# One pass over the weights for the output and query projections of a hybrid attention layer

## The chip, the core and the metric

The kernel runs on one core of one Trainium2 chip. A core has a matrix engine (TensorE, PE in the profile, with its weight loads as PEld), a vector engine (VectorE, DVE), a scalar engine (ScalarE, ACT), GpSimd (POOL) and SyncE (SP), whose queue issues most of the transfers. PE writes its results to PSUM, in banks of 512 float32 values per partition. The metric is the device time of one execution in microseconds.

## What is computed

The input is x, 2048 tokens of 1024 features. One layer is computed, with two token mixers beside each other:

```python
h = einsum("bsd,dc->bsc", x, w_in)                   # all input projections
qkv = silu(causal_short_conv(h[..., :1536], conv_w)) # branch A: gated DeltaNet, 4 heads of 128
o_a = chunked_gated_delta_rule(q_a, k_a, v_a, g, beta)
y_a = rmsnorm(o_a) * dn_norm_w * silu(dn_z)
q_b = partial_rope(sw_q); k_b = partial_rope(sw_k)   # branch B: 8 query heads of 64, window 128
y_b = banded_sink_attention(q_b, k_b, v_b, sinks) * silu(sw_z)
merged = sigmoid(gate_a) * (y_a @ w_branch[0]) + sigmoid(gate_b) * (y_b @ w_branch[1])
out = merged @ w_out
y = layer_norm(alpha * x + out) * ln_g + ln_b
```

The delta rule needs the inverse of a unit triangular matrix for each block of tokens.

## The kernel before

The 2048 tokens go through in four chunks of 512 (T), each of four blocks of 128. The order of pieces within a chunk stands in two strings, `ORDER_FIRST` for chunk 0 and `ORDER` for the others (L44, L45): "kv" and "w0", "w1" are the projections of window attention, "q0" to "v3" those of the delta rule's heads, "g" and "z" gates, and "p" a quarter of the output projection of the chunk before. So a chunk from the second on holds two query pieces (w0, w1) and four projections (p).

Every float32 product is made of three matmuls on high and low parts (`prods`, L173 to L175). Weights arrive in quarters of 512 columns as a pair of high and low parts in a buffer "wb". There are four such buffers (`W_SPLIT`). In the first use of a weight it is loaded raw, split by ScalarE and GpSimd (L154, L155) and stored back to DRAM as "kw_..."; later uses load that (L150). Where tokens are the rows of the result (`prod_tc`, L190), a quarter of the weights is the moving operand and a block of tokens the stationary one. Results stand in PSUM buffers "mm", of which there are three.

`window_q` (L538) makes the queries of four heads. It goes over its four quarters twice: first for blocks 0 and 1, then for blocks 2 and 3, each block in a PSUM buffer of its own, with the list `ww` keeping the quarters for the second pass. After each pass `rope` (L857) rotates the two blocks into SBUF tiles "kr" (a ScalarE copy, L861, and four VectorE instructions, L865 to L867), and `query_rows` (L557) is set up, which transposes them on PE (L562) into the tiles "qT". There are two "kr" buffers, so the second pair of blocks needs the transposes of the first: `st.finish("qT0")`. `project` (L666) likewise goes over its quarters twice, once for blocks 0 and 2 and once for 1 and 3, with two blocks in each of two banks.

The order on PE is written out by the program. Dense products come from generators that give their planned length (`PE_R`, 216 ns for 512 columns), and the class `Order` (L805) keeps a clock `now` of planned time. Dependent work is a task: `spawn` gives it a latency after which it may stand (`LAT_Q`, 7900 ns, for `query_rows`), and after each few products `run` puts down all tasks whose time has come. A task's step gives its own length and the latency until its next step. `finish(name)` (L834) runs tasks until one is done, and where none is ready it sets the clock forward to the next one's time:

```python
if name not in self.done:
    self.now = min(t[0] for t in self.tasks)
```

Tasks that matter here: `front` (L350; decay products L387, then the matrix m goes through DRAM to the tile "su"), `inverse` (VectorE, L904 to L916, result through DRAM to "p_", L423 and L435), `levels` (L426; its first matmuls on p_ are L447), and `back` (L472), the delta rule's recurrence: L494, then VectorE's bt (L496), L499 and L502, VectorE's wc (L501), L505 and L507, VectorE's S (L506), and so on for four blocks. The other engines' order is set by a scheduler.

Of the kernel before, what the change touches and what calls it, by code (L numbers as in the profile page):

```python
# [8 lines left out]
F32 = mybir.dt.float32  # L9
# [7 lines left out]
P = 128  # L17
D = 1024
KT = D // P
T = 512  # L20
NB = T // P
# [40 lines left out]
def build(tc, xt, xn, wk, wg, par, lnp, cst, out, seq=2048):  # L62
    nc = tc.nc
    NCH = seq // T
    with ExitStack() as ctx:
# [9 lines left out]
        sm = pool("sm", 2)  # L75
        mm = pool("mm", 3, space=PSUM)
# [5 lines left out]
        first = {}  # L82
        stage = lambda src: (lambda t: (nc.sync.dma_start(out=t, in_=src), t)[1])(ps_.tile([P, T], F32, name="s"))
        for n in ("x0", 0, "x1", 1, 2, "x2", "x3", 3, 4, 5, "x4", "x5", "x6", "x7"):
            if isinstance(n, str):
                k = int(n[1])
# [11 lines left out]
        cos = ct[:, C_COS:C_COS + P].rearrange("p (n e) -> p n e", e=8)  # L98
        sin = ct[:, C_SIN:C_SIN + P].rearrange("p (n e) -> p n e", e=8)
# [59 lines left out]
        def half_w(name, i, k=4, out=None):  # L159
            return [w.rearrange("p (k c) -> p k c", k=k) for w in split((name, i), wg[G_AT[name], :, 512 * i:512 * i + 512], 512, out)]  # L160

        def quarters(names):

            for name in names:
                for i in range(2):
                    yield half_w(name, i, 2)

        def prods(ps, terms, first=True, last=True):

            n = len(terms) - 1  # L170
            cost = PE_R * ps.free_size() / 512
            for i, (sh, sl, mh, ml) in enumerate(terms):
                nc.tensor.matmul(ps, sh, mh, start=(first and i == 0), stop=False)  # L173
                nc.tensor.matmul(ps, sh, ml, start=False, stop=False)  # L174
                nc.tensor.matmul(ps, sl, mh, start=False, stop=(last and i == n))  # L175
                if cost * 3 * (i % 2 + 1) > 1000 or i == n:
                    yield cost * 3 * (i % 2 + 1)

        def proj_ct(c, name):

            c.ps = mm.tile([P, T], F32, name="mm")
            for i in range(2):
                wh, wl = half_w(name, i)
                load_x(c, 4 * i + 3)
                yield from prods(c.ps, [(wh[:, k], wl[:, k], c.xh[4 * i + k], c.xl[4 * i + k]) for k in range(4)], i == 0, i == 1)

        def tok(a, b):
            return a[:, b * P:(b + 1) * P]

        def prod_tc(pss, blocks, ah, al, ww, load=None):  # L190

            for g, (wh, wl) in enumerate(ww):
                if load:
                    load(2 * g + 1)
                for ps, b in zip(pss, blocks):
                    yield from prods(ps, [(tok(ah[2 * g + k], b), tok(al[2 * g + k], b), wh[:, k], wl[:, k])
                                          for k in range(2)], g == 0, g == 3)

        def kept(ww, into):
            for w in ww:  # L200
                into.append(w)
                yield w

        def load_x(c, k):

            for k in range(len(c.xh), k + 1):
                if not k % 2:
                    c.pair = [px.tile([P, 2, T], F32R, name=n) for n in ("xh", "xl")]
                hi, lo = (t[:, k % 2] for t in c.pair)
                raw = pw.tile([P, 528], F32, name="w", bufs=W_RAW)[:, :512]  # L210
                nc.sync.dma_start(out=raw, in_=xt[c.i, :, k // 2, k % 2])
                nc.scalar.activation(hi, raw, AF.Copy)
                nc.vector.tensor_tensor(lo, raw, hi.bitcast(F32), ALU.subtract)
                c.xh.append(hi)
                c.xl.append(lo)
# [106 lines left out]
        def silu2(c, name):  # L322
            yield from proj_ct(c, name)
            while sum(n not in st.done for n in c.zs) >= 3:
                st.finish(next(n for n in c.zs if n not in st.done))
            c.zs.append(f"window{int(name[2]) // 2}" if name[0] == "z" else f"gate{name[1]}")
            r = ph.tile([P, T], F32, name="z", bufs=3)
            nc.scalar.activation(r, c.ps, AF.Tanh, scale=0.5)
            nc.vector.scalar_tensor_tensor(r, r, 1.0, c.ps, ALU.add, ALU.mult)
            c.z[name] = r  # L330
# [207 lines left out]
        def window_q(c, gp):  # L538

            if gp:  # L540
                st.finish("window0")
            c.qT = [pa.tile([P, NB, 2, P], F32R, name=n, bufs=1) for n in ("qT0", "qT1")]
            ww, more = [], quarters([f"q{gp}{i}" for i in range(2)])
            for b0 in (0, 2):
                pss = [mm.tile([P, T], F32, name="mm")[:, :256] for _ in range(2)]
                yield from prod_tc(pss, (b0, b0 + 1), c.xh, c.xl, ww if b0 else kept(more, ww), lambda k: load_x(c, k))
                if b0:
                    st.finish("qT0")
                qr = [pa.tile([P, 256], F32, name="kr") for _ in range(2)]
                for b, ps in enumerate(pss):  # L550
                    rope(nc, sm, qr[b], ps, 4, cos[:, c.i * NB + b0 + b], sin[:, c.i * NB + b0 + b])
                st.spawn(f"qT{b0}", query_rows(c, b0, qr), LAT_Q)
            for g in range(2):
                yield from silu2(c, f"zb{2 * gp + g}")
            st.spawn(f"window{gp}", attend(c, gp), LAT_W)

        def query_rows(c, b0, qr):  # L557

            pst = pp.tile([P, 2, 2, P], F32, name="pp")
            for b in range(2):  # L560
                for g in range(2):
                    nc.tensor.transpose(pst[:, b, g], tok(qr[b], g), ident)  # L562
            lo = pa.tile([P, 2, 2, P], F32, name="pT").bitcast(F32R)
            for v, vs_ in enumerate(HALF):
                q = c.qT[v][:, b0:b0 + 2]
                nc.scalar.activation(q[vs_], pst[vs_], AF.Copy)
                nc.vector.tensor_tensor(lo[vs_], pst[vs_], q[vs_].bitcast(F32), ALU.subtract)
                nc.gpsimd.dma_start(out=q[HALF[1 - v]], in_=lo[vs_])
            yield 4 * PE_T, 0
# [96 lines left out]
        def project(c, eg):  # L666

            if not eg:
                c.ra = [py.tile([P, 2, D], F32, name=n) for n in ("yBh", "yBl")]
            ww, more = [], quarters([f"o{eg}{i}" for i in range(2)])  # L670
            es = slice(256 * eg, 256 * eg + 256)
            xr, pss = [], [mm.tile([P, 2, 256], F32, name="mm") for _ in range(2)]
            for bp in range(2):
                xr.append(pa.tile([P, 2, 256], F32, name="s"))
                t0 = c.i * T + bp * 256
                nc.sync.dma_start(out=xr[bp], in_=xn[t0:t0 + 256, es].rearrange("(b p) e -> p b e", p=P))
            for b2 in range(2):
                yield from prod_tc([ps[:, b2] for ps in pss], (b2, 2 + b2), c.mh, c.ml, ww if b2 else kept(more, ww))
            for bp in range(2):
                nc.vector.scalar_tensor_tensor(c.ra[bp][:, :, es], xr[bp], 2.0 * ALPHA, pss[bp], ALU.mult, ALU.add)  # L680

# [97 lines left out]
        c = Chunk(0)  # L779
        for i in range(NCH):  # L780
# [20 lines left out]
            c = nxt  # L801
# [55 lines left out]
def rope(nc, sm, out, ps, heads, cos, sin):  # L857

    split = lambda a: a[:, :64 * heads].rearrange("p (h e) -> p h e", e=64)
    s, d = split(ps), split(out)  # L860
    nc.scalar.activation(d[:, :, 16:], s[:, :, 16:], AF.Copy)  # L861
    t = s[:, :, :16].rearrange("p h (r e) -> p h r e", e=8)
    a = sm.tile([P, 2, 4, 2, 8], F32, name="rope", bufs=1)[:, :, :heads]
    for i, f in enumerate((cos, sin)):
        nc.vector.tensor_tensor(a[:, i], t, f.unsqueeze(1).unsqueeze(1).to_broadcast([P, heads, 2, 8]), ALU.mult)  # L865
    nc.vector.tensor_tensor(d[:, :, 0:8], a[:, 0, :, 0], a[:, 1, :, 1], ALU.subtract)  # L866
    nc.vector.tensor_tensor(d[:, :, 8:16], a[:, 0, :, 1], a[:, 1, :, 0], ALU.add)  # L867
# [123 lines left out]
```

## Time and profile before

| | us |
|---|---|
| median of 3 timed runs | 1763.5 |
| lowest, highest | 1761.4, 1765.48 |
| the profiled execution | 1761.3 |
| its span | 1759.5 |
| PE busy | 1679.8 |
| DVE busy | 1020.6 |

"Busy" counts the time in which an engine's instructions run. Those of PE overlap, so the distance between two starts, not a duration, tells what one costs in a stream. A row in brackets tells how long the engine was idle before an instruction, and what ended that. The clock is the share of full speed that TensorE was granted.

### The profile page before, as it was taken

The numbers are of one execution on the slowest core, as the hardware profiler recorded it, in microseconds if no ns is written. First come the engines' busy times: TensorE is split into PE (matmuls) and PEld (weight loads), VectorE is DVE, ScalarE is ACT, GpSimd is POOL, SyncE is SP. The second block draws the span as 40 slices with busy tenths as digits, with TensorE's granted clock in tenths as the row PEclk, the third lists the DMA queues.
The fourth block names the chain that finished last, engine by engine and source line by source line (L and its number), as shares of the span: only waits on it lengthen the run. The fifth ranks groups of instructions, "written<-read, shape, count | busy, mean of one in ns | idle before, by whom it ended". The sixth has DMA issues, their size and how long they took to land.

```text
span 1759.5 us, 27318 instructions
## 1 busy us (share of the span) xinstructions
PE 1679.8 (95%) x9846; PEld 1389.3 (79%) x9846; DVE 1020.6 (58%) x3118; ACT 548.7 (31%) x1496; POOL 375.5 (21%) x364
## 2 busy tenths in 40 slices
PE   8999999899898999999989899999998899999997
PEld 6867877687886778778878678877888777877787
DVE  6667688356676656425547675733454857463245
ACT  3544444333232432231302243323130234332200
POOL 4533443441343111000104211000010511100001
PEclk9989999999999999999999999999999999999999
DMA  8855666676666455457565544646555554564762
GB/s 300 265 188 194 213 231 195 195 230 228 231 207 202 123 154 154 145 170 227 163 199 168 173 122 147 175 131 185 176 179 193 175 173 131 148 176 137 262 211 78
DMA packets 189159, 323.39 MB, mean 184 GB/s; under 512 B 31072, under 2 KB 45408, under 8 KB 188896
## 3 DMA queue, kind: packets, MB, share of 16 engines
q1 hardware_dynamic: 185184, 316.40, 56.6%
q0 software_dynamic: 3840, 5.25, 1.3%
q8 instruction: 78, 1.28, 0.3%
q14 instruction: 57, 0.47, 0.1%
HBM read 244.97 MB, written 71.37 MB: 180 GB/s over the span
## 4 chain that ended last, share of the span: by engine, by line
PE 77%; DVE 10%; DMA 7%; issue 2%; ACT 1%; POOL 1%; SPq 1%; POOLq 0%; ACTq 0%; DVEq 0%
PE mm L173 21%; PE mm L175 19%; PE mm L174 19%; DMA wb<-kw_o 2%; PE pp L587 2%; PE pp L586 2%; PE pp L625 2%; DVE kr L866 2%; DVE xt L915 2%; PE pp L617 2%; POOL wb L155 1%; PE pd L499 1%; DVE xi L916 1%; PE pd L505 1%; PE pd L387 1%
## 5 line engine op out<-in xcount | busy, mean ns | idle before, releaser
L173 PE MATMUL mm<-xh,wb 128*128 128x512 f32 x1128 | 477.0, 423 | 0.8 <-DMA wb<-kw_h 0.8
L175 PE MATMUL mm<-xh,wb 128*128 128x512 f32 x1128 | 446.9, 396 | 0.0
L174 PE MATMUL mm<-xl,wb 128*128 128x512 f32 x1128 | 445.9, 395 | 0.0
L175 PEld LDWEIGHTS mm<-xh,wb 128*128 128x128 f32 x1128 | 213.2, 189 | 50.4
L173 PEld LDWEIGHTS mm<-xh,wb 128*128 128x128 f32 x1128 | 214.1, 190 | 48.0 <-issue 5.9
L174 PEld LDWEIGHTS mm<-xl,wb 128*128 128x128 f32 x1128 | 215.1, 191 | 36.0
L155 POOL TENSOR_TENSOR wb<-w,wb 128x512 fp32r<-128x512 f32 (+1 forms) x110 | 150.0, 1367 | 192.0 <-ACT wb L154 171.7
L173 PE MATMUL mm<-wb,s 128*128 128x256 f32 x384 | 114.3, 298 | 17.7 <-DMA wb<-kw_o 13.0
L173 PE MATMUL mm<-wb,xh 128*128 128x256 f32 (+1 forms) x384 | 115.5, 301 | 9.9 <-DVE rope L865 4.2
L174 PE MATMUL mm<-wb,xh 128*128 128x256 f32 (+1 forms) x384 | 110.5, 288 | 0.8 <-POOL wb L155 0.8
L174 PE MATMUL mm<-wb,s 128*128 128x256 f32 x384 | 110.6, 288 | 0.0
L175 PE MATMUL mm<-wb,xl 128*128 128x256 f32 (+1 forms) x384 | 110.2, 287 | 0.0
L175 PE MATMUL mm<-wb,s 128*128 128x256 f32 x384 | 110.2, 287 | 0.0
L154 ACT ACTIVATE wb<-w 128x512 fp32r<-128x512 f32 (+1 forms) x110 | 68.8, 628 | 103.7 <-PE mm L175 55.8
L915 DVE TENSOR_TENSOR xt<-su,xi 128x16 f32<-128x16 f32 (+15 forms) x256 | 96.7, 378 | 5.5
L603 ACT ACTIVATE s<-s,nm 128x256 f32<-128x256 f32 (+1 forms) x128 | 62.7, 491 | 100.3 <-DVE nm L597 100.3
L173 PEld LDWEIGHTS mm<-wb,s 128*128 128x128 f32 x384 | 75.1, 196 | 21.7 <-DMA wb<-kw_o 15.1
L173 PEld LDWEIGHTS mm<-wb,xh 128*128 128x128 f32 x384 | 74.7, 195 | 13.3 <-issue 7.3
L916 DVE TENSOR_REDUCE xi<-xt 128x8 f32<-128x16 f32 (+15 forms) x256 | 74.7, 292 | 5.9
L174 PEld LDWEIGHTS mm<-wb,xh 128*128 128x128 f32 x384 | 74.7, 194 | 1.3 <-POOL wb L155 1.0
L174 PEld LDWEIGHTS mm<-wb,s 128*128 128x128 f32 x384 | 75.2, 196 | 0.3 <-POOL wb L155 0.2
L175 PEld LDWEIGHTS mm<-wb,s 128*128 128x128 f32 x384 | 75.0, 195 | 0.0
(668 smaller groups left out, 3195.9 us busy)
## 6 DMA issues: line engine op xcount, KB each, us to landing
wb<-kw_h SPq DMA_DIRECT2D x96, 512.0 KB, 4.1
wb<-kw_g SPq DMA_DIRECT2D x96, 512.0 KB, 4.0
w<-in_wg SPq DMA_DIRECT2D x106, 256.0 KB, 3.9
wb<-kw_b SPq DMA_DIRECT2D x48, 512.0 KB, 4.6
wb<-kw_o SPq DMA_DIRECT2D x36, 512.0 KB, 4.9
kw_h<-wb SPq DMA_DIRECT2D x32, 512.0 KB, 4.0
kw_g<-wb SPq DMA_DIRECT2D x32, 512.0 KB, 3.4
wb<-kw_q SPq DMA_DIRECT2D x24, 512.0 KB, 4.0
```

Source lines behind the costliest of these rows:

```text
L154: nc.scalar.activation(hi, raw, AF.Copy)
L155: nc.gpsimd.tensor_tensor(lo, raw, hi.bitcast(F32), ALU.subtract)
L173: nc.tensor.matmul(ps, sh, mh, start=(first and i == 0), stop=False)
L174: nc.tensor.matmul(ps, sh, ml, start=False, stop=False)
L175: nc.tensor.matmul(ps, sl, mh, start=False, stop=(last and i == n))
L586: nc.tensor.matmul(psc[v][:, g, k0:], c.qT[v][:, b, g], kT[v][:, ks], start=True, stop=False)
L587: nc.tensor.matmul(psc[v][:, g, k0:], c.qT[v][vs_, b, g], kT[2][vs_, ks], start=False, stop=True)
L603: nc.scalar.activation(s[:, g, k0:], s[:, g, k0:], AF.Exp, bias=nm[:, g:g + 1], scale=0.125, accum_out=su[:, g:g + 1])
L617: nc.tensor.transpose(psp[:, kb, g], ss[v][:, g, P * kb:P * kb + P], ident)
L625: nc.tensor.matmul(psY[64 * v:64 * v + 64], c.vs[b + kb][:, 64 * v:64 * v + 64], pTs[v][:, kb], start=(kb == kbs[0]), stop=(kb == 1))
L915: nc.vector.tensor_tensor(tx[:, :, :, :n], u, x, ALU.mult)
L916: nc.vector.tensor_reduce(xi[:, :, i:i + 2], tx[:, :, :, :n], AX.X, ALU.add)
```

## The change

A new helper, `prod_all`, goes over the quarters once. For each it makes the products of all four blocks, in the order 0, 2, 1, 3, into two banks of PSUM with two blocks each. Only the first block in a bank starts with the flag that clears it. `window_q` and `project` use it, and no quarter is kept for a second pass. In `window_q` the rotation of all four blocks now comes after all products. `prods` has a parameter that turns off a check for several open sums in one bank.

```diff
+        def prod_all(pss, ah, al, ww, load=None):
+
+            for g, (wh, wl) in enumerate(ww):
+                if load:
+                    load(2 * g + 1)
+                for b in (0, 2, 1, 3):
+                    yield from prods(pss[b // 2][:, b % 2], [(tok(ah[2 * g + k], b), tok(al[2 * g + k], b), wh[:, k], wl[:, k])
+                                                             for k in range(2)], g == 0 and not b % 2, g == 3, True)
...
             c.qT = [pa.tile([P, NB, 2, P], F32R, name=n, bufs=1) for n in ("qT0", "qT1")]
-            ww, more = [], quarters([f"q{gp}{i}" for i in range(2)])
+            pss = [mm.tile([P, 2, 256], F32, name="mm") for _ in range(2)]
+            yield from prod_all(pss, c.xh, c.xl, quarters([f"q{gp}{i}" for i in range(2)]), lambda k: load_x(c, k))
             for b0 in (0, 2):
-                pss = [mm.tile([P, T], F32, name="mm")[:, :256] for _ in range(2)]
-                yield from prod_tc(pss, (b0, b0 + 1), c.xh, c.xl, ww if b0 else kept(more, ww), lambda k: load_x(c, k))
                 if b0:
                     st.finish("qT0")
                 qr = [pa.tile([P, 256], F32, name="kr") for _ in range(2)]
-                for b, ps in enumerate(pss):
-                    rope(nc, sm, qr[b], ps, 4, cos[:, c.i * NB + b0 + b], sin[:, c.i * NB + b0 + b])
+                for b in range(2):
+                    rope(nc, sm, qr[b], pss[b0 // 2][:, b], 4, cos[:, c.i * NB + b0 + b], sin[:, c.i * NB + b0 + b])
                 st.spawn(f"qT{b0}", query_rows(c, b0, qr), LAT_Q)
...
-            ww, more = [], quarters([f"o{eg}{i}" for i in range(2)])
             es = slice(256 * eg, 256 * eg + 256)
...
-            for b2 in range(2):
-                yield from prod_tc([ps[:, b2] for ps in pss], (b2, 2 + b2), c.mh, c.ml, ww if b2 else kept(more, ww))
+            yield from prod_all(pss, c.mh, c.ml, quarters([f"o{eg}{i}" for i in range(2)]))
```

The change moves instructions on three engines. In the changed kernel line numbers are higher: 494 is 504, 499 is 509, 502 is 512, 505 and 507 are 515 and 517, 562 is 571, 586 and 587 are 595 and 596, 447 is 457.

PE, from the end of the second query piece of chunk 1 to the first level of a head's inverse (p_); mm 128x256 are the query products, mm 128x512 those of the pieces after it. Before:

```order
L494 MATMUL pd<-S,k 128x128
...
L175 MATMUL mm<-wb,xl 128x256
L562 MATMUL pp<-ct,kr 128x128 x4
L173 MATMUL mm<-xh,wb 128x512
...
L499 MATMUL pd<-bt,q__6562 128x128
L502 MATMUL pd<-S,qd 128x128
...
L505 MATMUL pd<-wc,ktl 128x128
L507 MATMUL pd<-wc,dt 128x128
...
L175 MATMUL mm<-xh,wb 128x512
L447 MATMUL pd<-p__7482,m_7098 32x32
```

and now:

```order
L176 MATMUL mm<-wb,xl 128x256
L504 MATMUL pd<-S,k 128x128
L509 MATMUL pd<-bt,q__6565 128x128
L512 MATMUL pd<-S,qd 128x128
L515 MATMUL pd<-wc,ktl 128x128
L517 MATMUL pd<-wc,dt 128x128
L504 MATMUL pd<-S,k 128x128
L571 MATMUL pp<-ct,kr 128x128 x4
L174 MATMUL mm<-xh,wb 128x512
...
L176 MATMUL mm<-xh,wb 128x512
L457 MATMUL pd<-p__7380,m_7085 32x32
```

Five steps of the recurrence and another L504 have moved together ahead of the transposes. From this head's decay products to its first level there were 60 products of 256 columns and 102 of 512, and now there are 60 and 72; the second query pieces of the other chunks have the same counts. For the head whose level follows the first query piece of chunks 1 to 3, there were 102 of 256 and 78 of 512, and now there are 102 and 54.

VectorE at the same place; su is the matrix that comes back through DRAM for the inverse. Before:

```order
L506 SCALAR_TENSOR_TENSOR S<-S,eGl,pd 128x128
L414 TENSOR_TENSOR dt<-pd,dt 128x512
L496 SCALAR_TENSOR_TENSOR bt<-pd,neG,vt 128x128
L904 MEMSET su 128x16
L907 TENSOR_TENSOR xt<-su 128x256
L908 TENSOR_TENSOR su<-su,xt 128x8x32
L865 TENSOR_TENSOR rope<-mm,ct 128x64 x2
L907 TENSOR_TENSOR xt<-su 128x256
L866 TENSOR_TENSOR kr<-rope 128x4x8
```

and now:

```order
L516 SCALAR_TENSOR_TENSOR S<-S,eGl,pd 128x128
L424 TENSOR_TENSOR dt<-pd,dt 128x512
L911 MEMSET su 128x16
L914 TENSOR_TENSOR xt<-su 128x256
L872 TENSOR_TENSOR rope<-mm,ct 128x64 x2
L915 TENSOR_TENSOR su<-su,xt 128x8x32
L506 SCALAR_TENSOR_TENSOR bt<-pd,neG,vt 128x128
L873 TENSOR_TENSOR kr<-rope 128x4x8
L874 TENSOR_TENSOR kr<-rope 128x4x8
```

The rope before is that of blocks 2 and 3 (those of 0 and 1 stood ahead of these rows); now it is that of blocks 0 and 1, and bt stands behind su's memset.

GpSimd, in the first query piece of chunk 1; yBh and yBl are the rows being normalized, L707 and L708 the layer norm's factor and offset, and the DMA rows carry qT to its other half. Before:

```order
L707 TENSOR_TENSOR yBh<-yBh,s 128x2x256
L707 TENSOR_TENSOR yBl<-yBl,s 128x2x256
L708 TENSOR_TENSOR yBh<-yBh,s 128x2x256
L568 DMA qT_5631<-pT 64x512
L707 TENSOR_TENSOR yBh<-yBh,s 128x2x256
L707 TENSOR_TENSOR yBl<-yBl,s 128x2x256
L708 TENSOR_TENSOR yBl<-yBl,s 128x2x256
L568 DMA qT_5632<-pT 64x512
```

and now (L714 and L715 are the layer norm, L577 the transfer):

```order
L714 TENSOR_TENSOR yBh<-yBh,s 128x2x256
L714 TENSOR_TENSOR yBl<-yBl,s 128x2x256
L714 TENSOR_TENSOR yBh<-yBh,s 128x2x256
L714 TENSOR_TENSOR yBl<-yBl,s 128x2x256
L715 TENSOR_TENSOR yBh<-yBh,s 128x2x256
L715 TENSOR_TENSOR yBl<-yBl,s 128x2x256
L715 TENSOR_TENSOR yBh<-yBh,s 128x2x256
L577 DMA qT_5627<-pT 64x512
```

The transfers of qT have moved behind the layer norm.

## Rows read from the trace of the kernel before

**Rows 1.** The page: engine busy time, share of the span and instructions

```profile
PE 1679.8 (95%) x9846; PEld 1389.3 (79%) x9846; DVE 1020.6 (58%) x3118; ACT 548.7 (31%) x1496; POOL 375.5 (21%) x364
```

**Rows 2.** Waits of PE: who, for whom, us in total, times, longest us

```profile
PE pd L499 <- DVE bt L496: 19.2, 6, 6.3
PE mm L173 <- DMA wb<-kw_o: 13.0, 8, 4.4
...
PE mm L173 <- DVE rope L865: 4.2, 3, 1.4
```

**Rows 3.** Stretches: length, busy us by engine, granted clock, DMA share, GB/s

```profile
890.70:897.50 6.80, 4.78 (x22) 4.78 (x23) 5.35 (x22) 0.00 (x0) 0.00 (x0) 0.50 0.01 5
1327.60:1330.95 3.35, 3.35 (x18) 3.35 (x17) 2.97 (x12) 0.00 (x0) 0.00 (x0) 0.50 0.03 5
522.05:525.40 3.35, 3.35 (x18) 3.35 (x18) 3.35 (x9) 0.00 (x0) 3.35 (x4) 0.50 0.38 113
542.55:545.90 3.35, 2.82 (x9) 2.43 (x10) 2.05 (x6) 0.00 (x0) 0.00 (x0) 0.50 0.14 32
...
1406.10:1412.90 6.80, 3.06 (x9) 2.67 (x10) 5.23 (x9) 0.00 (x0) 2.38 (x2) 0.50 0.14 32
```

**Rows 4.** Timeline of PE: start us, us, what; 512-column products in a stream

```profile
679.97 0.39 PE L173 MATMUL mm<-xh,wb 128*128 128x512 f32 x1
680.20 0.40 PE L174 MATMUL mm<-xl,wb 128*128 128x512 f32 x1
```

**Rows 5.** The page: transfers by tile, count, KB each, median us to landing

```profile
wb<-kw_o SPq DMA_DIRECT2D x36, 512.0 KB, 4.9
```

**Rows 6.** Timeline of ScalarE and VectorE, rope of blocks 0 and 1, chunk 1

```profile
664.38 0.33 ACT L861 ACTIVATE kr<-mm 128x192 f32<-128x192 f32 x1 [2.38 <-PE mm L175]
...
666.40 0.19 DVE L867 TENSOR_TENSOR kr<-rope 128x32 f32<-128x32 f32 x1
```

**Rows 7.** Line 435, loads of p_: duration min/median/max ns, first to last start

```profile
L435 SPq DMA_DIRECT2D p__2774<-scrp x4: 325/423/430, 243.1 to 244.4; - x4
...
L435 SPq DMA_DIRECT2D p__5898<-scrp x4: 333/422/430, 545.5 to 546.8; - x4
...
L435 SPq DMA_DIRECT2D p__7482<-scrp x4: 309/424/430, 701.0 to 702.3; - x4
...
L435 SPq DMA_DIRECT2D p__11675<-scrp x4: 308/426/430, 1135.8 to 1137.1; - x4
...
L435 SPq DMA_DIRECT2D p__15868<-scrp x4: 308/424/431, 1563.7 to 1565.0; - x4
...
DMA to landing us min/median/max: 1.5/2.9/5.1
```

**Rows 8.** Timeline of PE: first matmul of the first level, five heads

```profile
246.45 0.21 PE L447 MATMUL pd<-p__2774,m 32*32 32x32 f32 x1
...
551.70 0.21 PE L447 MATMUL pd<-p__5898,m 32*32 32x32 f32 x1
...
703.36 0.21 PE L447 MATMUL pd<-p__7482,m 32*32 32x32 f32 x1
...
1139.35 0.21 PE L447 MATMUL pd<-p__11675,m 32*32 32x32 f32 x1
...
1570.46 0.21 PE L447 MATMUL pd<-p__15868,m 32*32 32x32 f32 x1
```

**Rows 9.** Timeline at the end of the second query piece, chunk 2

```profile
1108.80 0.60 PE L562 MATMUL pp<-ct,kr 128*128 128x128 f32 x4
...
1110.97 0.07 DVE L904 MEMSET su<- 128x16 f32 x1 [2.35 <-DMA su<-scrm]
```

**Rows 10.** Timeline behind the first query piece, chunk 1

```profile
534.78 7.01 DVE L866 TENSOR_TENSOR kr<-rope 128x32 f32<-128x32 f32 x1
...
540.46 1.26 POOL L708 TENSOR_TENSOR yBl<-yBl,s 128x512 f32<-128x512 f32 x1
...
543.08 0.58 PE L499 MATMUL pd<-bt,q__4946 128*128 128x128 f32 x1 [5.80 <-DVE bt L496]
```

More of the change, by code (lines that the diff above doesn't have):

```diff
@@ L166, in quarters, with prods @@
                     yield half_w(name, i, 2)
-        def prods(ps, terms, first=True, last=True):
+        def prods(ps, terms, first=True, last=True, shared=False):
             n = len(terms) - 1
@@ L172, in prods @@
             for i, (sh, sl, mh, ml) in enumerate(terms):
-                nc.tensor.matmul(ps, sh, mh, start=(first and i == 0), stop=False)
-                nc.tensor.matmul(ps, sh, ml, start=False, stop=False)
-                nc.tensor.matmul(ps, sl, mh, start=False, stop=(last and i == n))
+                nc.tensor.matmul(ps, sh, mh, start=(first and i == 0), stop=False, skip_group_check=shared)
+                nc.tensor.matmul(ps, sh, ml, start=False, stop=False, skip_group_check=shared)
+                nc.tensor.matmul(ps, sl, mh, start=False, stop=(last and i == n), skip_group_check=shared)
                 if cost * 3 * (i % 2 + 1) > 1000 or i == n:
```

## The prediction

> **What bounds the kernel now.** I read the page's list of engines first: TensorE (PE) is busy 95% of the span, more than any other engine [rows 1]. So time is PE's work, which the change leaves alone (the same number of matmuls of the same widths), plus PE's idle time, plus what a lower clock costs. Next the waits of PE: 13.0 us for the stored output weights (kw_o) in 8 waits, 4.2 us for the rotary step (rope, L865) in 3, and 19.2 us for the delta rule's bt in 6, the longest 6.3 [rows 2]. Then the stretches by clock: after long waits PE runs for 3.4 to 6.8 us at a granted clock of 0.50, the lower of its two levels (1.2 against 2.4 GHz); I charge half of such a stretch [rows 3]. Last, single rows around the query pieces, which show what PE is about to wait for where it does not wait yet.
>
> **The projections (12 pieces in three chunks).** Nothing is added here; each quarter of weights is now used by 24 products in one stretch, not by 12 and 12. A 512-column product takes 0.23 us of PE's stream (two starts in [rows 4]), so I take 0.115 for 256 columns: 1.4 us per quarter and pass before, 2.8 after. Four buffers hold quarters. Before, the buffer that the second pass gives back must be full again three quarters later, 3 x 1.4 = 4.2 us, while the median landing is 4.9 us [rows 5]. After, it has 3 x 2.8 = 8.3 us. The longest of the 8 waits was 4.4 us, that is a landing of about 4.2 + 4.4 = 8.6: hidden but for 0.3. So the 13.0 us go, and with them the slow stretches that followed the two long waits, 6.80 and 3.35 us, worth 5.1 together [rows 3]. Term: -18. Bounds: -9 (half of it stays, since the same queue also carries the residual's and the delta rule's loads) to -22 (waits of this kind that carry another name go too).
>
> **What the change does to the query pieces.** Before, the rotary step of blocks 0 and 1 started after the first pass and ran under the second one, so the forced step `finish("qT0")` found it done. Now all four blocks end together, the step is spawned with 7.9 us of planned latency, and the next line forces it at once. The planner jumps its clock by that latency with nothing dense to fill it. Before, the jump was 2.7 us (7.9 less the 48 products that it plans at 108 ns). So everything that the planner holds moves up by 5.2 us against the dense work. The order shows both effects: five delta-rule steps now stand back to back before the transposes of qT, each needing VectorE's answer to the one before it; and 24 products (first query piece of chunks 1 to 3) or 30 (second piece of all four chunks) fewer stand between the decay products (L387) and the inverse's first level (L447).
>
> **First query piece of chunk 0.** PE waits for two ropes. In the trace two blocks took from the first ScalarE copy at 664.38 to the last kr instruction at 666.40, 2.2 us with its own time, which overlaps PE's last 0.7 us [rows 6]. Term: +2. Bounds: 0 (other steps fill it) to +5 (a slow stretch follows).
>
> **Second query pieces, four of them.** The level step needs p_, which comes back through DRAM after the inverse on VectorE. Its loads are issued last at 244.4, 702.3, 1137.1 and 1565.0 and land a median of 2.9 us later [rows 7]: 247.3, 705.2, 1140.0, 1567.9. PE arrived at 246.45, 703.36, 1139.35 and 1570.46 [rows 8]. So three had no slack at all and the fourth 2.6 us. Thirty products fewer are 30 x 0.23 = 6.9 us less cover. What p_ depends on starts at L387, whose place is unchanged, and its length is VectorE's and DRAM's, so PE must idle: 4 x 6.9 - 2.6 = 25 us. A second reading gives the same size: in chunk 2 the products of the piece ended by the transposes at 1108.80, but VectorE sat until 1110.97 for the load su [rows 9], and bt and the ropes now stand behind su's memset in VectorE's order. Two ropes more, 2.2 us, make the stall at least 4.4 us there; this stall is part of the 6.9, since both lie between L387 and L447. Bounds: +9 (the ropes alone, 4 x 2.2) to +34 (6.9 each with no slack, and 1.5 more for two ropes that now stand in the inverse's way). I take +25, by rows 7 and 8. For the clock: stalls of 1.40 to 6.3 us were followed by 3.35 to 6.80 us at 0.50 [rows 3], a cost of 1.7 to 3.4 each. I take 4 x 2.5 = +10, bounds 0 (no stretch falls) and +14.
>
> **First query pieces of chunks 1 to 3.** Here before pays already: 1.40 us each for the rope in the middle (a buffer of the second pass), 4.2 in all, then bt 5.80 us late [rows 2, 10], about 17.4 for the three. Slow stretches follow both: 3.35 us after each rope wait, and after bt 3.35 in chunk 1 and 6.80 in chunk 3, which I take for chunk 2 as well. Half of 4 x 3.35 + 2 x 6.80 is 13.5 [rows 3]. Together 35, or 11.7 a piece. The rope wait goes, since no buffer is needed in mid-piece. bt was late because VectorE's kr at 534.78 took 7.01 us, not 0.19: it ended as GpSimd's last layer-norm instruction did [rows 6, 10]. Two things are late next. The level step loses 24 x 0.23 = 5.5 us of cover, and in chunk 1 its slack was 551.70 - (546.8 + 2.9) = 2.0 [rows 7, 8]. If the 7 us come again, p_ comes when it did, and PE, freed of 7.2 us of waits and 3.4 of clock, idles 5.5 + 7.2 + 3.4 - 2.0 = 14.1 us where it paid 10.6: +3.5 and up to 1.7 of clock, +15 for three. If they do not, 7.1 of idle and 1.7 of clock: -1.8, -5 for three. I take +6, since GpSimd's order now has seven layer-norm instructions in a row there, with no transfer of qT between them, and kr and the inverse's products stand beside them.
>
> The Trainium skill says in "SBUF — State Buffer", Who interferes with whom, that a VectorE instruction with two SBUF inputs contends with a GpSimd instruction that reads SBUF, and that whoever comes first blocks the other for the whole instruction. By that rule kr would wait for one GpSimd instruction, about 1.3 us, and the term would be nearer -5 than +6. The row does not agree: 7.01 us spans several of them.
>
> **Sum.** -18 + 2 + 25 + 10 + 6 = +25 on the profiled execution's 1761.3 us (span 1759.5): 1786. The median of the timed runs is 1763.5, 2.2 higher, so I predict 1788 on their scale, 1.4% slower.
>
> **Rivals.**
> Worse: VectorE is held by GpSimd again and the ropes add to the inverse. -18 + 5 + 34 + 14 + 15 = +50, 1813. For it: kr's 7.01 us came in all three chunks. Against: PE's stalls leave VectorE less to do.
> The weights still wait: the projections gain nothing, because the wait was not the buffer but the queue before it. +43, 1806. Against: the loads' median landing fits the wait well.
> Faster: the hold of VectorE by GpSimd vanishes in all three first pieces, and p_ comes so early that only a short stall of 3 us and 1.7 of clock is left: -35 + 14 = -21 in place of +6, so -2; with the projections' full -22 it is -6, 1757. It decides once a first piece costs under 5 us. Against: even 7 us earlier p_ leaves 7.1 us of idle.
> No saving and no loss (the planner's jump costs nothing because delta-rule steps are short): then -18 + 2 + 9 + 0 - 5 = -12, 1751. Against: three slacks of zero.
>
> **How the numbers follow.** Forecast 0.62 (its own range 1773 to 1801), worse 0.17, weights still wait 0.06, faster 0.07, no loss 0.03; 0.05 lies between forecast and the faster cases, within 0.2% (3.5 us, about what a measurement of this kernel can tell from no change). So slower 0.85, same 0.05, faster 0.10. The range 1762 to 1815 leaves out the two faster cases and the tail above the worse one.
>
> **What would show it.** Right: no kw_o waits in the projections; PE idle before the five back-to-back steps and the transposes of qT, some 3 to 6 us in each second query piece, with bt, wc, S or kr as releasers; a further wait at the first level for p_ or for VectorE's transposes; stretches at 0.50 after them. Wrong: a second query piece in which PE goes from its last product to the first level with under 3 us of idle, or a p_ that lands more than 4 us sooner after L387 than before.

## The result, and the profile after

The changed kernel takes 1807.3 us (median of 4 runs, 1804.6 to 1811.0), against 1764.5 for the kernel before on the same chip: ratio 1.0242, 95% interval 1.0212 to 1.0272. It is slower, as forecast, but by 43 us where I had summed 25; it falls inside the stated range, but above the forecast's own case, which ended at 1801, and nearer the worse rival. The span of the profiled execution went from 1759.5 to 1806.8, 47.3 us more.

The page of the changed kernel, the line that answers to [rows 1]:

```profile
PE 1697.1 (94%) x9846; PEld 1404.8 (78%) x9846; DVE 1022.6 (57%) x3118; ACT 553.8 (31%) x1496; POOL 373.2 (21%) x364
```

The same 9846 matmuls are busy 17 us longer; the stretches below show a lower granted clock to go with it. The waits of PE in the changed kernel, with the columns of [rows 2]:

```profile
PE pd L509 <- DVE bt L506: 17.7, 10, 4.4
PE pd L504 <- DVE S L516: 10.9, 10, 2.8
PE pd L515 <- DVE wc L511: 9.8, 12, 3.1
PE pd L492 <- DVE v L329: 8.3, 3, 2.8
...
PE pp L457 <- DMA p__10049<-scrp: 4.0, 1, 4.0
PE pd L457 <- DMA p__2661<-scrp: 3.6, 1, 3.6
PE pp L457 <- DMA p__5860<-scrp: 3.5, 1, 3.5
PE pp L457 <- DMA p__14238<-scrp: 3.4, 1, 3.4
```

No row names kw_o or the rope any more. In their place the recurrence's steps wait one after the other (bt, wc, S), the first level waits for p_, and one wait is new to me: L492, the transposes of v with which `back` begins, once behind each first query piece of chunks 1 to 3.

Next I cut both traces at the same products, so that each piece can be compared with itself. A cut takes in what a piece hands on: the stretch of the first query piece (chunk 1) goes from its first product to 144 products past its end, that of the second one from its last quarter to 120 past its end, that of the projections (chunk 2) from the middle of the first one to the middle of the query piece behind them. Before (columns as in [rows 3]):

```profile
511.59:585.48 73.89, 66.13 (x399) 54.45 (x398) 54.49 (x157) 20.67 (x57) 28.09 (x26) 0.95 0.53 166
668.99:711.42 42.43, 42.43 (x266) 34.39 (x264) 29.93 (x111) 12.44 (x37) 3.71 (x6) 1.00 0.65 190
874.70:951.77 77.07, 69.72 (x545) 65.12 (x544) 39.43 (x118) 13.77 (x39) 11.17 (x12) 0.96 0.60 182
```

The same three in the changed kernel:

```profile
524.33:610.58 86.25, 70.45 (x403) 57.87 (x402) 54.38 (x159) 22.02 (x57) 27.37 (x26) 0.90 0.47 142
692.94:743.03 50.09, 46.68 (x280) 37.27 (x279) 31.27 (x120) 14.29 (x42) 3.87 (x7) 0.97 0.53 149
905.53:971.69 66.16, 66.16 (x546) 62.83 (x545) 38.83 (x118) 13.79 (x39) 11.14 (x12) 1.00 0.71 212
```

The projections' stretch is 10.9 us shorter and now runs without a gap at full clock. Those of the two query pieces are 12.4 and 7.7 us longer, with a lower clock in both. Over all pieces (idle is the sum of PE's waits in them, clock is half of the time at a granted 0.50; both traces, in us):

| pieces | predicted | measured | idle | clock |
|---|---|---|---|---|
| projections, chunks 1 to 3 | -18 | -19.9 | 17.7 to 4.9 | -6.8 |
| to the end of w0, chunk 0 | +2 | -0.7 | 9.7 to 8.9 | -1.7 |
| w1, four chunks, with the stretch ahead of each | +35 | +36.9 | 2.8 to 23.8 | +13.7 |
| w0, chunks 1 to 3 | +6 | +34.8 | 24.2 to 47.5 | +11.9 |
| rest | 0 | -3.8 | | |
| the whole span | +25 | +47.3 | | |

How much falls to a piece depends by some us on the cut: counted up to the first product of the second query piece, w0 comes to +32.2 and most of the rest is gone, since steps that now stand inside the stretch stood behind it before. Either way one term was mis-sized, that of w0 in chunks 1 to 3. There the stretches at half clock, which answer to the last three of [rows 3], are three in chunk 1 where there were two:

```profile
544.60:551.40 6.80, 4.63 (x15) 4.06 (x16) 6.77 (x18) 1.76 (x4) 5.63 (x6) 0.50 0.00 1
561.60:568.40 6.80, 4.72 (x26) 3.98 (x27) 2.28 (x5) 1.45 (x3) 0.56 (x2) 0.50 1.00 322
588.90:592.30 3.40, 3.40 (x10) 2.62 (x9) 0.32 (x1) 0.00 (x0) 0.00 (x0) 0.50 0.00 0
```

And the timeline of PE shows what stands ahead of each (the wait and its releaser are in the brackets, as in [rows 8, 10]):

```profile
540.51 0.49 PE L509 MATMUL pd<-bt,q__4935 128*128 128x128 f32 x2 [1.27 <-DVE bt L506]
543.23 0.49 PE L515 MATMUL pd<-wc,ktl 128*128 128x128 f32 x2 [2.01 <-DVE wc L511]
546.77 0.80 PE L504 MATMUL pd<-S,k 128*128 128x128 f32 x2 [2.83 <-DVE S L516]
559.97 0.24 PE L457 MATMUL pd<-p__5860,m 32*32 32x32 f32 x2 [2.06 <-DMA p__5860<-scrp]
563.68 0.26 PE L457 MATMUL pp<-p__5860,m 32*32 32x32 f32 x1 [3.46 <-DMA p__5860<-scrp]
587.86 0.63 PE L492 MATMUL pd<-ct,v 128*128 128x128 f32 x4 [2.78 <-DVE v L329]
```

The waits of this piece add up to 15.8 us. In the three pieces together, 22.1 of the 47.5 us are for bt, wc and S, 16.4 for p_ and 8.3 for v. In the second query piece of chunk 1, the loads of p_ and the first level (answering to [rows 7, 8]):

```profile
L445 SPq DMA_DIRECT2D p__7380<-scrp x4: 309/426/430, 724.0 to 725.3; - x4
```

```profile
725.56 0.24 PE L457 MATMUL pd<-p__7380,m 32*32 32x32 f32 x2 [0.30 <-DMA p__7380<-scrp]
```

From the head's decay products to the last landing of p_ it was 41.5 us before and 40.4 now: here p_ comes when it did, and PE arrives earlier. In the second pieces of chunks 0, 2 and 3 it is later: 39.5 to 45.4, 40.7 to 43.8, 38.6 to 41.5. The inverse itself, from its first to its last TENSOR_REDUCE, takes 21.0, 18.0, 18.2 and 17.8 us in chunks 0 to 3 where it took 19.9, 15.7, 15.6 and 15.6. The longest waits of PE in these pieces are for bt, ahead of the transposes: 12.6 us in the four, against 6.7 for p_.

What VectorE did in the first query piece of chunk 1, beside GpSimd's layer norm (timeline; the first four rows are VectorE's, the others GpSimd's):

```profile
532.06 0.16 DVE L923 TENSOR_REDUCE xi<-xt 128x8 f32<-128x16 f32 x1
...
543.49 1.30 DVE L874 TENSOR_TENSOR kr<-rope 128x32 f32<-128x32 f32 x1
...
547.39 1.46 DVE L922 TENSOR_TENSOR xt<-su,xi 128x224 f32<-128x224 f32 x1
...
554.36 0.41 DVE L923 TENSOR_REDUCE xi<-xt 128x8 f32<-128x256 f32 x1
...
543.48 1.26 POOL L714 TENSOR_TENSOR yBh<-yBh,s 128x512 f32<-128x512 f32 x1
...
547.28 1.32 POOL L715 TENSOR_TENSOR yBl<-yBl,s 128x512 f32<-128x512 f32 x1
```

The 7.01 us of [rows 10] is gone; no VectorE instruction takes over 1.5 us there. But seven take 1.3 to 1.5, and the inverse still takes 22.7 us (24.5 before).

### The profile page after: what moved, and what is told of

It reads as the page before. It is cut to its first block, busy times and chain, and to the rows that moved or that the text cites. A ratio compares the mean times of both kernels' runs of the same rounds, so it can differ in the third digit from the quotient of the medians.

```text
span 1806.8 us, 27278 instructions
## 1 busy us (share of the span) xinstructions
PE 1697.1 (94%) x9846; PEld 1404.8 (78%) x9846; DVE 1022.6 (57%) x3118; ACT 553.8 (31%) x1496; POOL 373.2 (21%) x364
## 4 chain that ended last, share of the span: by engine, by line
PE 76%; DVE 10%; DMA 8%; issue 3%; POOL 1%; ACT 1%; SPq 1%; POOLq 0%; ACTq 0%; DVEq 0%
PE mm L174 20%; PE mm L176 19%; PE mm L175 19%; DVE xt L922 2%; PE pp L596 2%; DMA su<-scrm 2%; PE pp L634 2%; PE pp L595 2%; PE pp L626 2%; DMA scrp<-xi 1%; POOL wb L155 1%; DVE xi L923 1%; PE pd L515 1%; PE pd L397 1%; PE pd L509 1%
## 5 line engine op out<-in xcount | busy, mean ns | idle before, releaser
L175 PE MATMUL mm<-xl,wb 128*128 128x512 f32 x1128 | 451.8, 401 | 0.0
L174 PEld LDWEIGHTS mm<-xh,wb 128*128 128x128 f32 x1128 | 218.3, 194 | 53.0 <-issue 7.8
L176 PEld LDWEIGHTS mm<-xh,wb 128*128 128x128 f32 x1128 | 217.0, 192 | 51.6
L175 PEld LDWEIGHTS mm<-xl,wb 128*128 128x128 f32 x1128 | 219.0, 194 | 39.0
L174 PE MATMUL mm<-wb,xh 128*128 128x256 f32 (+1 forms) x384 | 113.2, 295 | 5.7 <-DVE ba L272 3.1
L922 DVE TENSOR_TENSOR xt<-su,xi 128x16 f32<-128x16 f32 (+15 forms) x256 | 113.4, 443 | 6.2
L174 PE MATMUL mm<-wb,s 128*128 128x256 f32 x384 | 111.2, 290 | 4.9 <-DVE yBh L687 4.9
L175 PE MATMUL mm<-wb,xh 128*128 128x256 f32 (+1 forms) x384 | 108.7, 283 | 0.8 <-POOL wb L155 0.8
L175 PE MATMUL mm<-wb,s 128*128 128x256 f32 x384 | 109.0, 284 | 0.0
L176 PE MATMUL mm<-wb,s 128*128 128x256 f32 x384 | 108.6, 283 | 0.0
L174 PEld LDWEIGHTS mm<-wb,xh 128*128 128x128 f32 x384 | 72.6, 189 | 8.5 <-issue 6.6
L174 PEld LDWEIGHTS mm<-wb,s 128*128 128x128 f32 x384 | 73.2, 191 | 6.7 <-DVE yBh L687 5.1
L175 PEld LDWEIGHTS mm<-wb,xh 128*128 128x128 f32 x384 | 72.5, 189 | 1.3 <-POOL wb L155 1.0
L175 PEld LDWEIGHTS mm<-wb,s 128*128 128x128 f32 x384 | 73.1, 190 | 0.1
L176 PEld LDWEIGHTS mm<-wb,s 128*128 128x128 f32 x384 | 73.2, 191 | 0.0
```

What stands on the lines that cost most here:

```text
L175: nc.tensor.matmul(ps, sh, ml, start=False, stop=False, skip_group_check=shared)
L922: nc.vector.tensor_tensor(tx[:, :, :, :n], u, x, ALU.mult)
```

## The experiments

In all the tables "w0" is the sum over the first query pieces of chunks 1 to 3, "w1" over the second ones of all chunks, each against the profiled kernel before, as in the table above. They come from one profiled execution each, which can lie some us from the median beside it (e4_zero_latency 4.7 above, e10_small_jump 5.9 below).

**The two parts, each alone.** `e1_project_alone` keeps the old query pieces, `e2_query_alone` the old projections (edits against the changed kernel).

```diff
-            yield from prod_all(pss, c.xh, c.xl, quarters([f"q{gp}{i}" for i in range(2)]), lambda k: load_x(c, k))
...
+                yield from prod_tc(pss, (b0, b0 + 1), c.xh, c.xl, ww if b0 else kept(more, ww), lambda k: load_x(c, k))
```

> Only the output projections go over their weights once; the query pieces keep their two passes. If the parts of the change add up piece by piece, as the drift between the two traces says (projections of chunks 1 to 3 together 20.1 us shorter), this takes 1764.5 - 20 = 1744 us (1740 to 1750), with no wait of PE for kw_o left. Rival: the projections' saving only moved a wait to the next piece, or came from the query pieces being late: then within 4 us of 1764.5.

```diff
-            yield from prod_all(pss, c.mh, c.ml, quarters([f"o{eg}{i}" for i in range(2)]))
...
+            for b2 in range(2):
+                yield from prod_tc([ps[:, b2] for ps in pss], (b2, 2 + b2), c.mh, c.ml, ww if b2 else kept(more, ww))
```

> Only the query pieces go over their weights once; the projections keep two passes. If the parts add up, 1807.3 + 20 = 1827 us (1820 to 1834), with the 13 us of kw_o waits back. Rival: the two parts disturb each other (the single pass of the projections is what starves the query pieces, through the weight queue or GpSimd), and the query pieces alone cost less: below 1815.

Measured: 1743.5 us (ratio to before 0.9873, 0.9858 to 0.9888) and 1826.1 (1.0341, 1.0324 to 1.0359). -22 and +61 from 1765.2 make +39 together; the whole change made +43. Both times lie in their theories' ranges: the parts add to within 4 us, and the projections' one pass by itself is a kernel that beats both. By piece, the queries alone gave w0 +33.8 and w1 +33.4. The projections of chunk 2 in e1_project_alone:

```profile
877.75:946.56 68.81, 66.66 (x545) 62.92 (x544) 40.10 (x126) 13.80 (x39) 11.12 (x12) 1.00 0.65 197
```

**The jump.** Three kernels take away the planner's jump, or make it smaller. `e3_no_jump` gives the rotated blocks 2 and 3 a tile of their own, so that nothing is forced:

```diff
                 if b0:
-                    st.finish("qT0")
-                qr = [pa.tile([P, 256], F32, name="kr") for _ in range(2)]
+                    qr = pa.tile([P, 2, 2, P], F32, name="pT").rearrange("p b g t -> p b (g t)")
+                    qr = [qr[:, b] for b in range(2)]
+                else:
+                    qr = [pa.tile([P, 256], F32, name="kr") for _ in range(2)]
```

> As the changed kernel, but the queries of blocks 2 and 3 are rotated into a free tile of the same size (pT), so that nothing has to be forced: the planner's clock is not set forward and no step of the recurrence is pulled up. The ropes of all four blocks still come together at the end of the piece. Theory: the jump causes the loss of the query pieces (34.5 us in the first pieces of chunks 1 to 3, 40.4 in the second ones), so most of the 75 go, and with the projections' 20 the time is 1735 to 1750. Rival: the loss is VectorE's, since four ropes at once stand in the way of the inverse and of bt while GpSimd's layer norm holds VectorE; then p_ still lands late, the first pieces keep most of their 34.5 us, and the time is 1765 to 1790.

`e4_zero_latency` and `e10_small_jump` keep the force and change the latency that the clock jumps by:

```diff
-                st.spawn(f"qT{b0}", query_rows(c, b0, qr), LAT_Q)
+                st.spawn(f"qT{b0}", query_rows(c, b0, qr), LAT_Q if b0 else 0)
```

> As the changed kernel, but the step that is forced has a planned latency of 0: it is put down at once, the planner's clock does not move, and no other step is pulled up. PE really waits for two ropes before the transposes in each of the eight query pieces, with nothing to fill it. Theory (the cover that the jump takes is the cost): PE waits some 3 us in each of 8 pieces and runs a stretch at half clock behind each, worth 2 more, 40 in all; the waits for p_, bt, wc and S of the changed kernel go, so 1744 + 40 = 1784 (1770 to 1795). Rival (the wait for the ropes is the cost and the pulled-up steps only stand where PE would wait anyway): no gain, 1800 to 1815.

```diff
-                st.spawn(f"qT{b0}", query_rows(c, b0, qr), LAT_Q)
+                st.spawn(f"qT{b0}", query_rows(c, b0, qr), LAT_Q if b0 else 2700)
```

> The changed kernel with a planned latency of 2700 ns in place of 7900 for the step that is forced (that of blocks 2 and 3 keeps 7900), so that the planner's clock jumps by at most 2.7 us, as in the kernel before. Theory: the cover in dense products is then that of before, the second query pieces lose only the real wait for two ropes (2 to 4 us each with its clock, as at latency 0), and the time lies near that of latency 0: 1768 to 1785. Rival: every jump of the clock costs in proportion, a third of the 32.5 us between latency 0 and the changed kernel: 1786; if the size of the jump does not matter, 1800 to 1807.

| | us | ratio to before | w0 | w1 |
|---|---|---|---|---|
| changed kernel | 1807.3 | 1.0242 | +34.8 | +36.9 |
| e3_no_jump | 1769.7 | 1.0022 (1.0007 to 1.0037) | +11.7 | +16.4 |
| e4_zero_latency | 1774.8 | 1.0053 (1.0034 to 1.0073) | +9.1 | +20.6 |
| e10_small_jump | 1771.4 | 1.0034 (1.0014 to 1.0055) | +2.8 | +22.1 |

All three give back 32 to 38 us, so the jump costs that much, and a jump of 2.7 us shows no cost beyond that of 0. Latency 0 and the small jump came out in their theories' ranges. The theory of e3_no_jump (1735 to 1750) did not: its time is the rival's, though not by the rival's mechanism, since no wait for p_ is left in w0 or w1, and w0 keeps 11.7 of 34.8. The waits that stand there now are others. Without the force, the scores wait for the transfers of qT, and wc is late:

```profile
PE pp L597 <- DMA qT<-pT: 22.1, 11, 3.8
PE pd L515 <- DVE wc L511: 14.0, 7, 3.9
```

With latency 0, the transposes wait for the ropes, which was priced at 3 us a piece; it is 33.3 us over the eight pieces, but 6.7 a piece in the first pieces of chunks 1 to 3 and 2.8 in the second ones:

```profile
PE pp L571 <- DVE kr L874: 33.3, 15, 4.7
```

`e5_no_jump_later_scores` was to remove the first of these, by letting the step of e3_no_jump count as done 6 us later:

```diff
-            yield 4 * PE_T, 0
+            yield 4 * PE_T, 6000
```

> As the kernel without the jump (1769.7 us), but the step that transposes the queries counts as done only 6 us after it (its last latency 6000 ns in place of 0), so that the scores of the window attention no longer stand right behind the transfers of qT. That kernel still waited 22.1 us for these transfers in 11 waits, each near a stretch at half clock. Theory: these waits are all that kept it above the 1744 us of the projections alone: 1769.7 - 22 - 4 to 12 of clock = 1736 to 1746, no wait for qT over 1 us. Rival: the waits only move on to the recurrence (wc, S, bt behind VectorE's ropes), or to p_, and the time stays at 1755 to 1770.

It took 1766.8 us (1.0014, 0.9999 to 1.0028). The rival was right: the scores still wait for qT, and wc is waited for as before.

```profile
PE pp L597 <- DMA qT<-pT: 16.2, 8, 3.4
PE pd L515 <- DVE wc L511: 13.7, 9, 3.9
```

**GpSimd's hold of VectorE.** Three kernels leave out most of the layer norm's factor and offset: they apply them to 2 of 256 columns in chunks 0 to 2, with either form of the query pieces and with or without the jump (the same edit in all):

```diff
-                    nc.gpsimd.tensor_tensor(r, r, lg[:, 0:1].to_broadcast([P, 2, 256]), ALU.mult)
-                    nc.gpsimd.tensor_tensor(r, r, lg[:, 1:2].to_broadcast([P, 2, 256]), ALU.add)
+                    nc.gpsimd.tensor_tensor(r[:, :, :2], r[:, :, :2], lg[:, 0:1, :2].to_broadcast([P, 2, 2]), ALU.mult)
+                    nc.gpsimd.tensor_tensor(r[:, :, :2], r[:, :, :2], lg[:, 1:2, :2].to_broadcast([P, 2, 2]), ALU.add)
```

> The changed kernel with the layer norm's factor and offset on GpSimd applied to 2 of every 256 columns only (chunks 0 to 2), so that these 16 instructions per chunk take next to nothing; the rest is as in the changed kernel. It asks how much of the 34.5 us that the first query pieces of chunks 1 to 3 lost is GpSimd's hold on VectorE. Theory: with no hold the inverse's chain of 49 us there is as short as in the second pieces (40 to 45), p_ lands 5 to 8 us earlier, and the bt, wc and S waits shrink: 15 to 30 us less than the changed kernel, 1777 to 1792. Rival: the loss is the steps pulled up by the jump alone, whatever GpSimd does: 1800 to 1807.

> The kernel before with the same cut of the layer norm on GpSimd (2 of every 256 columns). If the hold of VectorE by GpSimd is what made bt late in the first query pieces (5.8 to 6.3 us in three chunks, 17.9 together, and a slow stretch behind each, 8.5), these waits go: 1764.5 - 18 to 26 = 1738 to 1747. Rival: bt waits for the rope and the inverse's products, not for GpSimd: within 5 us of 1764.5.

> The kernel with the forced step at latency 0 (1774.8 us, no jump), and GpSimd's layer norm again on 2 of every 256 columns only. With the jump this cut gave 31.7 us (1807.3 to 1775.6), in the kernel before 9.5. Theory: the jump and GpSimd's hold cost what they do in the first query pieces only together, since either the cover or the shorter inverse is enough to hide it; then without the jump the cut gives as little as before: 1774.8 - 5 to 13 = 1762 to 1770. Rival: the two costs add, and the cut gives 31.7 again: 1740 to 1747.

| us | whole norm | cut norm | difference | w0, whole to cut |
|---|---|---|---|---|
| kernel before | 1765.4 | 1755.9 | -9.5 | 0 to -9.4 |
| changed, with the jump | 1807.3 | 1775.6 | -31.7 | +34.8 to +2.6 |
| changed, latency 0 | 1774.8 | 1741.5 | -33.3 | +9.1 to -21.4 |

Ratios to before of the three: 0.9940 (0.9917 to 0.9963), 1.0059 (1.0035 to 1.0082), 0.9878 (0.9853 to 0.9904). With the jump, the cut norm gave a little more than its theory had (15 to 30). My theory for the last was wrong: the hold and the jump add. In w0 the hold costs 32.2 with the jump and 30.5 without, the jump 25.7 with the hold and 24.0 without.

The first query piece of chunk 1 in the changed kernel with the cut norm:

```profile
526.64:601.74 75.10, 66.82 (x403) 55.04 (x402) 42.01 (x159) 21.95 (x57) 9.25 (x26) 0.95 0.53 162
```

VectorE does the same 159 instructions in 42.01 us instead of 54.38. In its timeline, rows that answer to those above:

```profile
532.81 0.16 DVE L923 TENSOR_REDUCE xi<-xt 128x8 f32<-128x16 f32 x1
...
540.40 0.18 DVE L874 TENSOR_TENSOR kr<-rope 128x32 f32<-128x32 f32 x1
...
541.79 0.39 DVE L922 TENSOR_TENSOR xt<-su,xi 128x224 f32<-128x224 f32 x1
...
546.24 0.42 DVE L923 TENSOR_REDUCE xi<-xt 128x8 f32<-128x256 f32 x1
```

The inverse takes 13.8 us, not 22.7, and in the three first pieces p_ lands 38.5 to 41.9 us after the decay products, not 49.0 to 49.4. PE's waits in this kernel:

```profile
PE pd L509 <- DVE bt L506: 10.5, 7, 3.0
...
PE pd L515 <- DVE wc L511: 4.4, 11, 1.0
...
PE pd L504 <- DVE S L516: 1.5, 6, 0.3
```

In w0 alone, the waits for bt, wc and S fall from 22.1 to 3.0 us and the clock's cost from 25.6 to 10.2, while that for p_ hardly moves (16.4 to 14.2): p_ comes sooner, but so does PE. The cut norm also frees GpSimd's own time, and the transfers of qT that it issues go out some 9 us sooner in the piece; but PE waits for none of them in the changed kernel, so that is not where the 32 us come from.

In the kernel before, the cut norm takes the inverse from 24.5 to 13.9 as well, and bt's 19.2 us of waits [rows 2] go to 1.3; why that is worth only 9.5 us, where the theory had 18 to 26, shows in that kernel's waits:

```profile
PE mm L173 <- DMA wb<-kw_zb: 18.6, 3, 6.3
...
PE pd L499 <- DVE bt L496: 1.3, 3, 0.4
```

A wait for the weights of the next piece took bt's place. SyncE's queue says why:

```profile
528.64 0.38 SPq L711 DMA_DIRECT2D out<-yBh  x1
529.12 0.42 SPq L711 DMA_DIRECT2D out<-yBl  x1
529.59 4.74 SPq L150 DMA_DIRECT2D wb<-kw_zb  x4
```

The norm ends early, so the two stores of a chunk's output now stand ahead of kw_zb, whose first load is issued at 529.59; in the kernel before kw_zb went out from 522.81 on and the stores at 548.57 and later. In the changed kernel with the cut norm the stores are early too, but its one pass gives a buffer back sooner (the first load is issued 3.3 us after the piece's first product, against 11.2 in the kernel before), and two of the four loads are ahead of them:

```profile
529.98 0.52 SPq L150 DMA_DIRECT2D wb<-kw_zb  x1
...
534.47 0.53 SPq L150 DMA_DIRECT2D wb<-kw_zb  x1
539.08 0.38 SPq L718 DMA_DIRECT2D out<-yBh  x1
```

By this reading the hold costs the kernel before about 28 us too (the 9.4, and the 18.6 that hide the rest), near what it costs the changed one. That is an estimate: no run takes the wait for kw_zb away.

`e8_norm_on_vector` puts both instructions on VectorE, on top of e5_no_jump_later_scores:

```diff
-                    nc.gpsimd.tensor_tensor(r, r, lg[:, 0:1].to_broadcast([P, 2, 256]), ALU.mult)
+                    nc.vector.tensor_tensor(r, r, lg[:, 0:1].to_broadcast([P, 2, 256]), ALU.mult)
...
```

> As e5_no_jump_later_scores, but with the layer norm's factor and offset on VectorE instead of GpSimd (16 instructions of 128x512 per chunk for three chunks; VectorE's instruction of that width took 0.68 us at the residual). If GpSimd's hold costs more than the work itself, VectorE has 11 us more to do in a chunk but no 7 us hold: 5 to 15 us faster than e5. Rival: the 11 us stand in front of bt and the inverse, which are on PE's path there: 5 to 20 us slower than e5.

1761.5 us (0.9973, 0.9959 to 0.9987), 5 us faster than its base, at the low end of the first theory. The wc waits shrink from 13.7 to 3.2, and p_ is late instead: ten of the norm's instructions, of 0.69 us each, now stand inside the inverse, which takes 23.9 to 26.7 us where its base had 21.2:

```profile
PE pd L457 <- DMA p__5890<-scrp: 8.5, 1, 8.5
PE pd L457 <- DMA p__14264<-scrp: 7.9, 1, 7.9
PE pd L457 <- DMA p__10077<-scrp: 6.1, 1, 6.1
```

**A better version?** `e11_two_passes_one_bank` is e1_project_alone with both blocks of a query pass in one bank, so that no buffer is short in mid-piece (edit against e1_project_alone; the part left out lets `prod_tc` put two blocks in a bank, as `prod_all` does):

```diff
-                pss = [mm.tile([P, T], F32, name="mm")[:, :256] for _ in range(2)]
+                bank = mm.tile([P, 2, 256], F32, name="mm")
+                pss = [bank[:, b] for b in range(2)]
...
```

> The projections in one pass (1743.5 us), the query pieces in two passes as before, but the two blocks of a pass in one bank of PSUM, so that a piece takes two of the three buffers and its second pass need not wait for the first rope. Theory: the three waits of 1.40 us for the rope and half of the 3.35 us stretch behind each go, and bt is no later for it: 1743.5 - 3 x (1.4 + 1.7) = 1734, range 1731 to 1740. Rival: PE only arrives sooner at bt, which GpSimd's hold sets, and waits there 1.4 us longer in each piece: 1741 to 1746.

1745.3 us (0.9889, 0.9871 to 0.9907), no better than 1743.5: the rival was right. The rope's waits (3.9 us in three) went, and PE waits for bt 5.1 us more in all, in chunk 1 in two places (2.17 is new):

```profile
531.48 0.53 PE L509 MATMUL pd<-bt,q__4935 128*128 128x128 f32 x2 [2.17 <-DVE bt L506]
546.08 0.58 PE L509 MATMUL pd<-bt,q__4935 128*128 128x128 f32 x1 [4.22 <-DVE bt L506]
```

## Why the prediction was right in sign and short in size

**Projections, -18: right.** Measured -19.9 in the pieces, and -22 as a kernel of its own. The waits for kw_o went with the slow stretches behind them.

**Second query pieces, +35: right in size, by the mechanism only in part.** 21.0 of idle against 25 and 13.7 of clock against 10. PE idles where I said, before the transposes and at the first level. But idle rose by 8.0, 3.4, 5.6 and 4.0 in chunks 0 to 3, where I had 6.9, 6.9, 6.9 and 4.3, so it is luck that the sum fits better than the pieces do. p_ comes when it did in chunk 1 alone; in the others it lands 2.9 to 5.9 us later, and the inverse takes 1.1 to 2.6 longer, with ropes beside it, which I had only in the upper bound. In chunk 1 PE idles 2.45 us before it starts the first level, less than the 3 that I had named as a sign of being wrong (3.41 with the wait inside that level). And the jump does not explain all of it: latency 0 gives back 16 of the 37 and leaves 20.6, with 11.3 of waits for the ropes and 5.1 of clock in place of the waits for bt and p_.

**First query piece of chunk 0, +2.** Measured -0.7: PE has no wait for the ropes there, other steps fill that time, and 3.4 us less run at half clock.

**First query pieces of chunks 1 to 3, +6: the term that was mis-sized.** I set +15 if GpSimd holds VectorE again and -5 if not, and took +6 between them: I saw seven layer-norm instructions in a row beside kr and the inverse, but priced the hold by the one row of 7.01 us. Measured: +34.8. Two things in this step were wrong.
First, the hold. The cut norm shows it to be worth 32 us here, and it does not hang on that row: without it the term is +2.6, inside my two cases, though not the -5 that I had for it. I had read one long instruction, and not that VectorE is busy 12 us more than its work takes in the whole piece. When that row vanished, the same time was spread over the inverse, the ropes and the recurrence: p_ came after 49.2 us, as before (49.0), and bt, wc and S were each late ahead of it.
Second, the clock in the case that the hold comes again. Idle time rose by 7.8 us a piece, where that case had 14.1 - 7.2 = 6.9. But I let the clock fall back by 3.4, since the two waits of before would go, and added at most 1.7. It rose by 4.0 a piece: the waits for bt, wc and S, those for p_ and the new one for v stand 13 to 24 us apart, and a stretch at 0.50 began at or behind each of the three groups. So the case had the idle time nearly right, 6.9 for 7.8, and lost its size at the clock: 7.8 + 4.0 = 11.8 a piece is the 35 measured for three.

The worse rival, +50 in all, had this mechanism (the hold again, and ropes in the inverse's way), but with the same +15 for these pieces and its surplus in others. "No saving and no loss" falls, since the jump costs 33 us; "the weights still wait" and "faster" fall with the waits of the projections and of p_.

**Left open.** v's wait goes with the jump (2.78 us in each of these pieces with the jump of 7.9 us, none at latency 0 or with the small jump). With the cut norm it is there too, and a slow stretch follows it in one piece of three, against three of three in the changed kernel; why is not shown. Of bt's 12.6 us in the second pieces, no run tells how much is owed to its place behind su's memset. What is left in w0 without the jump has several causes: in their traces e3_no_jump waits 13.8 us there for wc and 11.1 for qT, e4_zero_latency 20.1 and e10_small_jump 13.9 for kr. No run takes them away one by one.

## What to carry to other kernels

In this kernel one pass over the weights was worth its whole wait where nothing depends on the piece's middle (the projections), and cost more than that where the middle fed a step that now has to be forced: compare the distance to the next dependent step before and after in dense products. When a planner's clock jumps, count every task that it pulls up, and look for groups of waits that stand apart: here three in a piece cost the clock three times, not once. And where an engine is slowed beside another, compare an instruction's time with the same one elsewhere, and sum over the piece: the longest row is only where the hold showed.

## What the runs showed of the hardware

The same VectorE product (128x224, two inputs in SBUF) took 1.46 us beside GpSimd's layer norm and 0.39 without it; the rope's kr 1.30 and 0.18; GpSimd's own instruction 1.26 to 1.43. So each takes 1.1 us longer here, a little less than one GpSimd instruction. The Trainium skill says in "SBUF — State Buffer", Who interferes with whom, that of two such instructions the one that comes first blocks the other for the whole instruction. The trace of the changed kernel agrees with that, though the term did not come out near the -5 that I had worked out from it: I had priced one held kr, and in chunk 1 seven VectorE instructions took 1.3 us or more. The 7.01 us of the kernel before, five times as long, does not. The same kr took 5.72 us in e1_project_alone and 2.93 in e4_zero_latency. What made one instruction wait for several is not shown by any run.
